# Hymba block with PEER experts: gates applied to more blocks at each build, more activations computed ahead, the mixer's output projection by pairs of tiles

## The chip, the cores and the metric

The kernel runs on one core of a Trainium2 chip. The metric is the time of one execution on the device, in microseconds (us). Times shown are medians of a few runs; the profile is of one execution.

## What is computed

One decoder layer on 512 tokens of width 1024, in float32:

```
h = rmsnorm(x);  z = h @ w_in                 # columns of 4 gated-delta heads and 4 mLSTM heads
mixed = concat(gated_delta(z), mlstm(z))      # each causal, by chunks; 8 heads of 128
x = x + mixed @ w_out                         # the mixer's output projection
h = rmsnorm(x);  x = x + attention(h @ wq, keys(mem), values(mem)) @ wo      # 4 heads, 256 memory tokens
h = rmsnorm(x)                                # PEER: 128*128 experts of one neuron each
q = h @ pwq                                   # 8 heads, two halves of 128 each
per head: scores of both halves against 128 keys, the top 16 of each half, the top 16 of the sums
gate = softmax(the 16 scores)                 # 8*16 = 128 experts for each token
x = x + sum(gate * gelu(h . u[expert]) * v[expert])
out = rmsnorm(x)
```

## The kernel before, in words

The 512 tokens are four tiles of 128. The stages follow each other: the mixer over all four tiles, its output projection (`residual(tiles, hs, "wout")`), cross-attention (`xattn`), and PEER. From the projection on, the order in which code is emitted is a string, ORDER_XA, whose words are run by the loop near the end of the file: `n` norms, `q` query blocks, `s` and `x` the attention's softmax and mix, `o` its output, `i` the norm and queries of PEER, `f` and `u` scores, `r R t T` routing (top 16), `k` and `b B` what follows routing, `p5` five gathered rows, `a2` two activations ahead. Each engine then keeps its own queue, in order.

A projection (`proj`) loads a weight tile of 128x1024 (512 KB) into one of two buffers, splits it into a high part (ACT, line 236) and a low part (DVE line 223 or POOL line 221, by the list `low_on`), and multiplies three times (high by high, high by low, low by high). `projT` is the same with the weights stationary. Where an activation is kept unsplit (`"f"`), the product runs on whole float32 (line 313).

PEER is done in two ways at the same time. Tiles 0 and 1 gather: for each of a token's 128 experts, one indirect DMA on POOL (line 1073) fetches a row of `u` for all 128 tokens (512 KB), and DVE reduces it against the token (line 1100); later the same with rows of `v` (line 1111). That is 512 rows in all. Tiles 2 and 3 are dense: for each of the 128 blocks of 128 experts, PE multiplies by the block of `u` (`pa`, an activation, line 313, then Gelu on ACT, line 972), the result is multiplied by a gate for every expert and token, and PE multiplies by the block of `v` (`o`, line 1000). The rows of the gather, the blocks of `u` (`in_pt`) and those of `v` (`in_pv`) come from HBM.

The gates of the dense tiles are 128 experts x 128 x 256 tokens, mostly zero. `build` makes them for 16 tokens at a time: DVE compares (line 934) and multiplies (line 940), PE multiplies the result (`acc`, line 945), ACT puts it into a `stage` (line 946). There are 16 builds. The dense blocks come in 16 groups of eight, and `room` has place for six groups, so 47 activations (`ahead`, word `a`) can run before the first `o`. After a build, `apply` (line 953) multiplies its gates into the first NOW = 2 groups where they stand; the gates of the other 14 groups are written to a DRAM tensor (`gates_`), and read again in the dense loop, a megabyte a group (line 992), and multiplied there by DVE (line 997).

In the dense loop (`peer_dense`) every step issues the loads of the coming blocks and then runs 3.15 gathered rows while activations are left (ROWS_BOTH), and 2.3 after that (ROWS_DOWN). At the end the gathered tiles are closed first on DVE (lines 1088 to 1091), then the dense ones (lines 1056 to 1066).

Of the kernel before, what the change touches and what calls it, by code (L numbers as in the profile page):

```python
# [6 lines left out]
F32 = mybir.dt.float32  # L7
# [9 lines left out]
P = 128  # L17
# [14 lines left out]
ROWS_BOTH, ROWS_DOWN = 3.15, 2.3  # L32
# [23 lines left out]
ORDER_XA = ("w2 n0 q008 n1 s0 x0 s1 x1 q104 o0 w1 i0 q148 f0 f1 r6 "  # L56
            "f2 s2 p2 f3 s3 p4 x2 p3 r3 p2 r3 k0 x3 p4 o1 p8 i1 e0 R3 p4 R3 p2 R4 k1 "
            "u0 p5 u1 p5 u2 p5 a1 u3 p5 a2 "
            + "t2 p4 a1 " * 4 + "t2 p4 a9 T2 p4 " + "b1 p5 a1 T2 " * 4 + "b1 p5 a8 d0 " + "b1 p5 a2 " * 3
            + "B1 p5 a1 " * 6 + "a1 p5 B1 p5 B1 p5 a6 ")  # L60
# [15 lines left out]
def _body(ctx, tc, A, out, dbg):  # L76
# [245 lines left out]
    def bank():  # L322
        return psB.tile([P, 512], F32, name="acc")

    def bank4():
        return psB.tile([P, 4, P], F32, name="acc")
# [36 lines left out]
    def gates(ph, wk, hs, tiles):  # L363
# [58 lines left out]
        for i in range(n):  # L422
# [8 lines left out]
        return {ti: dict(beta=beta[:, i], cum=cum[:, i], enm=enm[:, i], br=br[:, i], cj=cj[:, i], beg=beg[:, i])  # L431
                for i, ti in enumerate(tiles)}

    def gdn(wk, items, gs, qkv, mixed):
# [15 lines left out]
        bc = bank4()  # L450
        for i, (h, ti) in enumerate(items):
            PE.matmul(bc[:, i], sel[:, h], gs[ti]["br"][:, 0], start=True, stop=True)
            c = gs[ti]["cum"][:, h:h + 1]
            V.scalar_tensor_tensor(ET[:, i], bc[:, i], c, maskT, op0=OP.subtract, op1=OP.add)
            V.scalar_tensor_tensor(EG[:, i], bc[:, i], c, maskP, op0=OP.subtract, op1=OP.add)
# [99 lines left out]
    def mlstm(wk, items, gs, qk, va, mixed):  # L555
# [3 lines left out]
        def wt(name, bufs=1):  # L559
            return wk.tile([P, n, P], F32, name=name, bufs=bufs)  # L560
        ET, es = wt("ET", 2), wt("eg", 2)
        for i, (h, ti) in enumerate(items):
            bc = bank()
            PE.matmul(bc[:, :256], sel[:, h], gs[ti]["br"][:, 1:3].rearrange("p a b -> p (a b)"),
                      start=True, stop=True)
            V.scalar_tensor_tensor(ET[:, i], bc[:, 128:256], gs[ti]["cj"][:, h:h + 1], maskT,
                                   op0=OP.add, op1=OP.add)
            SC.activation(es[:, i], bc[:, 0:128], AF.Exp)
# [30 lines left out]
    def mixer(tiles, aside):  # L599
        nt = len(tiles)  # L600
        with tc.tile_pool(name="mxp", bufs=nt) as ph, tc.tile_pool(name="mxw", bufs=2) as wk:
# [89 lines left out]
            residual(tiles, hs, "wout")  # L691
# [11 lines left out]
    def xattn():  # L703
# [4 lines left out]
        wr = row(1, wpool, name="wh")  # L708
# [18 lines left out]
        def query(g, blocks):  # L727
            def ev(nb, ps):
                SC.activation(qT[:, nb, cols(g)], ps, AF.Copy)
            if "f" in part(g):  # L730
                projected(part(g)["f"], len(g), A["wq"], blocks, ev)
            else:
                projT(part(g), len(g), A["wq"], blocks, ev)
# [187 lines left out]
    NOW = 2  # L921
# [5 lines left out]
    def build(t0, bufs, stage, bank):  # L927

        for s in range(0, TG, TS):
# [9 lines left out]
            for a in range(TS // Q):  # L939
# [3 lines left out]
                for k in range(Q):  # L943
                    for g in range(2):
                        PE.matmul(ps[:, k], oj[:, a, :, k], og[:, g, a, :, k], start=g == 0, stop=g == 1)  # L945
                SC.activation(stage[:, :, s + a * Q:s + a * Q + Q], ps.rearrange("p t i -> p i t"), AF.Copy, scale=1.0 / GSCALE)
        nc.scalar.dma_start(gates_[:, :, t0 // TG].rearrange("g p i t -> p g (i t)"),
                            stage[:, NOW * GB:].rearrange("p (g i) t -> p g (i t)", i=GB))

        def apply():  # L950
            for g in range(NOW):
                a = room[g][:, :, t0:t0 + TG]
                V.tensor_tensor(a, a, stage[:, g * GB:(g + 1) * GB], op=OP.mult)  # L953
        fresh.append(apply)

    fresh = []
# [9 lines left out]
    room, count_a = [], [0]  # L966
# [7 lines left out]
    def peer_dense(wu, psO, psC, rest):  # L974
# [15 lines left out]
        def gates_of(g):  # L990
            if g < NKEY // GB:
                G.dma_start(gb[:, g % 3], gates_[g - NOW])

        def gated(g):

            a = room[g % NROOM].rearrange("p e (c t) -> p c e t", t=TG)
            V.tensor_tensor(a, a, gb[:, g % 3], op=OP.mult)
# [137 lines left out]
    t = late.tile([P, 2, DB, 2 * P], F32R, name="dh0")  # L1135
    dh.append({"h": t[:, 0], "l": t[:, 1]})
    t = late.tile([P, 4, D], F32, name="dh1")
    dh.append({"f": eight(t), "room": t})
# [8 lines left out]
    for a in range(K):  # L1147
        G.memset(rows_[:, 0, a], float(start[a]))
        G.memset(rows_[:, 1, a], float(start[a] - start[a - 1] if a else 0))
        G.memset(rows_[:, 2, a], float(a))  # L1150
# [46 lines left out]
    for what in ORDER_XA.split():  # L1197
# [3 lines left out]
        elif kind == "q":  # L1201
            n, x, y = (int(c) for c in what[1:])
            query(GS[n], range(x, y))
        elif kind == "s":
# [26 lines left out]
        elif kind == "f":  # L1231
            first.scores(n)
        elif kind == "u":
            second.scores(n)
        elif kind == "e":
            t = late.tile([P, 6, D], F32, name="W0")
            room.extend(blocks(t[:, k:k + 2]) for k in (0, 2, 4))
            room.append(blocks(first.room[:, 0:2]))
        elif kind == "d":
            del rings[-6:-2]  # L1240
            room.extend(blocks(more[:, k:k + 2]) for k in (0, 2))
        elif kind == "a":
            ahead(n)
        elif kind == "k":
            ready[G0[n]] = first.finish(G0[n], slot)
        elif kind == "p":
            run(gather, n)
        else:
            if kind not in flows:
                i, f = {"r": (0, 0), "R": (1, 0), "t": (0, 0), "T": (1, 0), "b": (0, 1), "B": (1, 1)}[kind]  # L1250
                g = first if kind in "rR" else second
                flows[kind] = settle(g, g.tiles[i]) if f else g.route(g.tiles[i], spot, 2 if kind == "r" else 1)
            run(flows[kind], n)
# [72 lines left out]
```

## Time and profile before

| | |
|---|---|
| median of 3 runs | 1864.69 us (1860.12 to 1868.1) |
| the profiled execution | 1863.43 us |
| its span, first to last instruction | 1861.5 us |
| mean granted TensorE clock | 0.957 |
| PE busy | 1682.0 us (90%) |
| DVE busy | 1248.2 us (67%) |
| POOL busy | 849.9 us (46%) |
| ACT busy | 393.9 us (21%) |
| moved by DMA | 514.81 MB, mean 277 GB/s |

The busy times are sums over the whole span, in which the stages have different limits: no engine's share says what a stage waits for. For that the view of the windows is read, which gives busy times and the bytes moved in each stretch of the span, and the views of the waits.

### The profile page before, as it was taken

The numbers are of one execution on the slowest core, as the hardware profiler recorded it, in microseconds if no ns is written. First come the engines' busy times: TensorE is split into PE (matmuls) and PEld (weight loads), VectorE is DVE, ScalarE is ACT, GpSimd is POOL, SyncE is SP. The second block draws the span as 40 slices with busy tenths as digits, with TensorE's granted clock in tenths as the row PEclk, the third lists the DMA queues.
The fourth block names the chain that finished last, engine by engine and source line by source line (L and its number), as shares of the span: only waits on it lengthen the run. The fifth ranks groups of instructions, "written<-read, shape, count | busy, mean of one in ns | idle before, by whom it ended". The sixth has DMA issues, their size and how long they took to land.

```text
span 1861.5 us, 21345 instructions
## 1 busy us (share of the span) xinstructions
PE 1682.0 (90%) x7444; PEld 1240.6 (67%) x7444; DVE 1248.2 (67%) x2767; ACT 393.9 (21%) x784; POOL 849.9 (46%) x686
## 2 busy tenths in 40 slices
PE   4999999999799986996998979993899999999993
PEld 3787777787698863885887746662666666664441
DVE  5656655473422598999998876557666566566668
ACT  5433442564243121111222210000000000000000
POOL 2121111323312044567344656666666666666663
PEclk9999999999899988998999979997999999999997
DMA  4111111234524477999799999999999999999996
GB/s 138 63 57 35 57 40 46 69 102 149 168 88 162 149 261 269 350 335 372 259 332 408 367 385 410 410 410 410 410 410 410 409 410 409 410 409 409 409 411 257
DMA packets 165355, 514.81 MB, mean 277 GB/s; under 512 B 15616, under 2 KB 44416, under 8 KB 163456
## 3 DMA queue, kind: packets, MB, share of 16 engines
q0 software_dynamic: 76608, 286.30, 39.3%
q1 hardware_dynamic: 59712, 212.48, 30.9%
q10 hardware_dynamic: 28928, 14.68, 2.7%
q8 instruction: 58, 0.95, 0.2%
q14 instruction: 49, 0.40, 0.1%
HBM read 494.52 MB, written 18.87 MB: 276 GB/s over the span
## 4 chain that ended last, share of the span: by engine, by line
DMA 38%; PE 33%; DVE 19%; issue 4%; POOL 3%; ACT 2%; SPq 0%; DVEq 0%; POOLq 0%; ACTq 0%
PE pj L313 7%; PE pj L271 7%; DMA row<-in_pv,ids 7%; PE pj L284 6%; DMA W<-in_pv,ids 6%; DMA Vm<-in_pv,ids 5%; PE acc L445 4%; DMA row<-in_pu,ids 3%; DMA wl<-in_pv,ids 3%; DMA W<-gates__132 3%; PE acc L945 2%; DMA gates__132<-W 2%; DVE W L1100 2%; DMA wl<-in_pu,ids 2%; DMA KT<-in_pv,ids 1%
## 5 line engine op out<-in xcount | busy, mean ns | idle before, releaser
L1000 PE MATMUL o<-ld,W 128*128 128x512 f32 x832 | 370.9, 596 | 4.6 <-DVE W L953 4.6
L313 PE MATMUL pa<-dh,ld 128*128 128x256 f32 x1296 | 295.5, 381 | 34.7 <-ACT dh L972 34.2
L313 PEld LDWEIGHTS pa<-dh,ld 128*128 128x128 f32 x1296 | 247.3, 191 | 103.1 <-issue 38.2
L1000 PEld LDWEIGHTS o<-ld,W 128*128 128x128 f32 x832 | 158.8, 191 | 175.7 <-issue 167.3
L221 POOL TENSOR_TENSOR wl<-w,wh 128x1024 fp32r<-128x1024 f32 x38 | 92.4, 2434 | 348.8 <-ACT wh L236 294.7
L313 PE MATMUL pj<-dh,w 128*128 128x256 f32 x704 | 161.3, 383 | 0.0
L313 PEld LDWEIGHTS pj<-dh,w 128*128 128x128 f32 x704 | 133.4, 193 | 17.8 <-ACT dh L294 0.3
L1073 POOL DMA_INDIRECT W<-in_pu,ids x73 | 95.4, 1307 | 91.0 <-DVE W L1100 52.2
L1111 DVE SCALAR_TENSOR_TENSOR dh<-row,act,dh 128x1024 f32<-128x1024 f32 x72 | 92.5, 1284 | 53.8 <-DMA row<-in_pv,ids 53.5
L1073 POOL DMA_INDIRECT row<-in_pu,ids x74 | 98.5, 1331 | 64.4 <-issue 17.8
L1073 POOL DMA_INDIRECT row<-in_pv,ids x74 | 99.9, 1351 | 47.2 <-issue 17.9
L313 PE MATMUL pj<-dh 128*128 128x256 f32 x496 | 113.2, 383 | 0.0
L284 PE MATMUL pj<-hT,wh 128*128 128x512 f32 x320 | 111.9, 421 | 0.0
L972 ACT ACTIVATE W<-pa 128x256 f32<-128x256 f32 x65 | 25.0, 384 | 407.2 <-PE pa L313 397.5
L271 PE MATMUL pj<-wh,hT 128*128 128x512 f32 x320 | 106.1, 404 | 0.4 <-ACT hT L211 0.4
L1100 DVE SCALAR_TENSOR_TENSOR row<-row,dh 128x1024 f32<-128x1024 f32 x74 | 88.3, 1223 | 22.4 <-DMA row<-in_pu,ids 22.1
L313 PEld LDWEIGHTS pj<-dh 128*128 128x128 f32 x496 | 94.5, 193 | 12.6
L1100 DVE SCALAR_TENSOR_TENSOR W<-W,dh 128x1024 f32<-128x1024 f32 x73 | 88.4, 1221 | 17.2 <-DMA W<-in_pu,ids 17.2
L236 ACT ACTIVATE wh<-w 128x1024 fp32r<-128x1024 f32 x56 | 59.3, 1059 | 124.2 <-PE pj L271 64.1
L1000 PE MATMUL o<-ld,dh 128*128 128x512 f32 x192 | 85.2, 592 | 0.0
L1073 POOL DMA_INDIRECT wl<-in_pu,ids x41 | 56.6, 1380 | 49.1 <-DVE tv L783 18.6
L1073 POOL DMA_INDIRECT wh<-in_pu,ids x40 | 54.2, 1354 | 49.9 <-DVE wh L1100 22.3
(431 smaller groups left out, 3106.5 us busy)
## 6 DMA issues: line engine op xcount, KB each, us to landing
ld<-in_pv SPq DMA_DIRECT2D x128, 512.0 KB, 6.8
ld<-in_pt SPq DMA_DIRECT2D x81, 512.0 KB, 6.9
gates__132<-W ACTq DMA_DIRECT2D x16, 896.0 KB, 13.9
W<-gates__132 POOLq DMA_DIRECT2D x14, 1024.0 KB, 17.1
w<-in_pt SPq DMA_DIRECT2D x24, 512.0 KB, 6.9
dh<-in_pt SPq DMA_DIRECT2D x23, 512.0 KB, 6.9
w<-in_win SPq DMA_DIRECT2D x20, 512.0 KB, 3.5
w<-in_pwq SPq DMA_DIRECT2D x16, 512.0 KB, 4.7
```

Of the source, the lines that this page charges most:

```text
L221: G.tensor_tensor(out, a, hi, op=OP.subtract)
L236: SC.activation(hi, wt, AF.Copy)
L271: PE.matmul(acc[i], a[:, d, i * P:(i + 1) * P], b[:, z], start=d == 0 and m == 0, stop=d == DB - 1 and m == len(pairs) - 1)
L284: PE.matmul(acc[:, :n * P], a[:, d], b[:, d], start=d == 0 and m == 0, stop=d == DB - 1 and m == 2)
L313: PE.matmul(ps, w[:, d], h[:, d], start=d == 0, stop=d == DB - 1)
L445: PE.matmul(ps[:, i], l[:, i], r[:, i], start=True, stop=True)
L945: PE.matmul(ps[:, k], oj[:, a, :, k], og[:, g, a, :, k], start=g == 0, stop=g == 1)
L972: SC.activation(place(e), ps, AF.Gelu)
L1000: PE.matmul(outs[DENSE[i]][z], place(e)[:, i * P:(i + 1) * P], v[:, z * 512:(z + 1) * 512], start=e == 0, stop=e == NKEY - 1)
L1073: G.indirect_dma_start(out=row, out_offset=None, in_=A[table], in_offset=bass.IndirectOffsetOnAxis(ap=ids[:, s:s + 1], axis=0))
L1100: V.scalar_tensor_tensor(row, row, 1.0, hn, op0=OP.mult, op1=OP.mult, accum_out=act[ti][:, s:s + 1])
L1111: V.scalar_tensor_tensor(hn, row, w, hn, op0=OP.mult, op1=OP.add)
```

## The change

What it does, piece by piece:

- The mixer's output projection runs for tiles 0 and 1 and then for tiles 2 and 3, with the weights loaded and split once for each pair; all low parts there are made by DVE.
- The norm's weight row in `xattn` comes by POOL's queue into a part of another tile, no longer by SP's.
- The query of tiles 2 and 3 is projected with split operands (`projT`) like that of tiles 0 and 1, and stands before the word `i0`.
- The 48 memsets of `row_numbers` move from the start of `xattn` to the word `f0`.
- 24 activations are called for before the first build (16 before); rows are called for six at a build (five before), and 169 in all before the last `apply` is done (158 before).
- `apply` multiplies a build's gates into every group whose eight activations are there: three groups, then four, then five, where it was two. Only what is not applied is written to `gates_` and read again, 188 pieces of 64 KB each way, where it was 224.
- In the mixer, one matmul for all four tiles spreads a head's gate row (line 452 of before) where there were four, and two where there were four of double width (line 564); one Exp stands for four.
- ROWS_BOTH and ROWS_DOWN become 3.1 and 2.1.

```diff
-ROWS_BOTH, ROWS_DOWN = 3.15, 2.3
+ROWS_BOTH, ROWS_DOWN = 3.1, 2.1
...
-ORDER_XA = ("w2 n0 q008 n1 s0 x0 s1 x1 q104 o0 w1 i0 q148 f0 f1 r6 "
+ORDER_XA = ("w2 n0 q008 n1 s0 x0 s1 x1 q104 o0 w1 q148 i0 f0 f1 r6 "
...
-            + "t2 p4 a1 " * 4 + "t2 p4 a9 T2 p4 " + "b1 p5 a1 T2 " * 4 + "b1 p5 a8 d0 " + "b1 p5 a2 " * 3
-            + "B1 p5 a1 " * 6 + "a1 p5 B1 p5 B1 p5 a6 ")
+            + "t2 p4 a2 " * 4 + "t2 p4 a6 T2 p4 a7 " + "b1 p6 a2 T2 " * 4 + "d0 " + "b1 p6 a2 " * 4
+            + "B1 p6 a1 " * 2 + "B1 p6 " * 6 + "a5 ")
...
         bc = bank4()
+        PE.matmul(bc[:, :n], sel[:, items[0][0]], gs["br"][:, :, 0], start=True, stop=True)
         for i, (h, ti) in enumerate(items):
-            PE.matmul(bc[:, i], sel[:, h], gs[ti]["br"][:, 0], start=True, stop=True)
...
-            residual(tiles, hs, "wout")
+            low_on[:] = [V]
+            for k in range(0, nt, 2):
+                residual(tiles[k:k + 2], {z: t[:, :, k * P:(k + 2) * P] for z, t in hs.items()}, "wout")
...
-        wr = row(1, wpool, name="wh")
+        wr = row_(1, up[:, 5], G)
...
-            if "f" in part(g):
-                projected(part(g)["f"], len(g), A["wq"], blocks, ev)
-            else:
-                projT(part(g), len(g), A["wq"], blocks, ev)
+            projT(part(g), len(g), A["wq"], blocks, ev)
...
-    NOW = 2
+    NOW = 3
...
-        nc.scalar.dma_start(gates_[:, :, t0 // TG].rearrange("g p i t -> p g (i t)"),
-                            stage[:, NOW * GB:].rearrange("p (g i) t -> p g (i t)", i=GB))
+
+        n = count_a[0] // GB
+        for g in range(n, NKEY // GB):
+            held[g] = t0 // TG + 1
+        nc.scalar.dma_start(gates_[n - NOW:, :, t0 // TG].rearrange("g p i t -> p g (i t)"),
+                            stage[:, n * GB:].rearrange("p (g i) t -> p g (i t)", i=GB))
 
         def apply():
-            for g in range(NOW):
-                a = room[g][:, :, t0:t0 + TG]
-                V.tensor_tensor(a, a, stage[:, g * GB:(g + 1) * GB], op=OP.mult)
+            for g, k, t in wide:
+                k = min(n - g, k) * GB
+                if k > 0:
+                    a = t[:, :k, t0:t0 + TG]
+                    V.tensor_tensor(a, a, stage[:, g * GB:g * GB + k], op=OP.mult)
...
-                G.dma_start(gb[:, g % 3], gates_[g - NOW])
+                G.dma_start(gb[:, g % 3, :held[g]], gates_[g - NOW, :, :held[g]])
```

Three places show how instructions stand on an engine before and after.

**DVE in the mixer's output projection.** `x<-pj` (line 699, then 700) adds a finished block of a tile to the residual, `wl<-w,wh` (line 223) is the low part of a weight tile. Before:

```order
L212 TENSOR_TENSOR hT<-tr,hT 128x4x128 x8
L223 TENSOR_TENSOR wl<-w,wh 128x1024
L699 TENSOR_TENSOR x<-pj,x 128x512 x4
L223 TENSOR_TENSOR wl<-w,wh 128x1024
L699 TENSOR_TENSOR x<-pj,x 128x512 x4
```

After:

```order
L212 TENSOR_TENSOR hT<-tr,hT 128x4x128 x5
L223 TENSOR_TENSOR wl<-w,wh 128x1024 x2
L700 TENSOR_TENSOR x<-pj,x 128x512
L223 TENSOR_TENSOR wl<-w,wh 128x1024
L700 TENSOR_TENSOR x<-pj,x 128x512
L223 TENSOR_TENSOR wl<-w,wh 128x1024 x3
L700 TENSOR_TENSOR x<-pj,x 128x512
```

The low parts, most of which POOL made before, now stand on DVE between the additions, four for each block of a pair, the first of them behind an addition that waits for PE.

**The norm's weight row, between the projection and the queries.** `wl<-w,wh` (line 221) belongs to the projection, `W<-w,W` and `W<-wl,W` to the query's weights, `in_nrow` is a norm's weight row. Before, POOL has the 48 memsets at this place, and the weight row is on SP's queue, ahead of a load of the query's weights:

```order
L246 DMA w<-in_wout 128x1024 x6
L246 DMA w<-in_wq 128x1024 x2
L246 DMA wl<-in_wq 128x1024
L191 DMA wh<-in_nrow 128x1024
L246 DMA wl<-in_wq 128x1024
```

After, on POOL:

```order
L221 TENSOR_TENSOR wl<-w,wh 128x1024 x11
L191 DMA W_4067<-in_nrow 128x1024
L221 TENSOR_TENSOR W_4065<-w,W_4065 128x1024
L221 TENSOR_TENSOR W_4065<-wl,W_4065 128x1024
L221 TENSOR_TENSOR W_4065<-w,W_4065 128x1024
```

The memsets are gone from here; a load has come in their place, into memory that the projection's operands held until then.

**DVE at the builds.** `KT` and `Vm` are a build's operands, `W<-W,W` is `apply`, `act<-…` is a gathered row. Before, two builds apart by five rows:

```order
L953 TENSOR_TENSOR W_5757<-W_5757,W_4107 128x8x16 x2
L940 TENSOR_TENSOR Vm<-Vm,slot 128x2x512 x2
L1100 SCALAR_TENSOR_TENSOR row,act_5297<-row,dh_4764 128x1024
L1100 SCALAR_TENSOR_TENSOR wh,act_5297<-wh,dh_4764 128x1024
L1100 SCALAR_TENSOR_TENSOR wl,act_5297<-wl,dh_4764 128x1024
L1100 SCALAR_TENSOR_TENSOR wh,act_5297<-wh,dh_4764 128x1024
L1100 SCALAR_TENSOR_TENSOR wl,act_5297<-wl,dh_4764 128x1024
```

After, at the first builds:

```order
L957 TENSOR_TENSOR W_5913<-W_5913,W_4067 128x24x16
L938 TENSOR_TENSOR Vm<-Vm,slot 128x2x512 x2
L932 TENSOR_TENSOR KT<-ioq,slot 128x1024 x2
L932 TENSOR_TENSOR Vm<-ioq,slot 128x1024
L938 TENSOR_TENSOR KT<-KT,slot 128x2x512 x2
L932 TENSOR_TENSOR Vm<-ioq,slot 128x1024
L957 TENSOR_TENSOR W_5913<-W_5913,W_4067 128x24x16
L938 TENSOR_TENSOR Vm<-Vm,slot 128x2x512 x2
L932 TENSOR_TENSOR KT<-ioq,slot 128x1024
```

Before, 80 rows stand ahead of the first build and 155 ahead of the last; after, 102 and 165, and the first four builds have no row between them. Each `apply` is one instruction on three groups (128x24x16) and, later, one or two more on one group. On PE, 24 activations stand ahead of the first build's transposes where there were 16, and behind the last `o` that is mixed with builds there follow four builds with nothing between, where there were two.

## Rows read from the trace of the kernel before

**Rows 1.** Windows: us, busy us of PE, PEld, DVE, ACT, POOL, granted clock, DMA share, GB/s.
```profile
800.00:850.00 50.00, 50.00 (x241) 44.24 (x240) 50.00 (x223) 6.55 (x16) 31.39 (x31) 1.00 0.95 357
...
1250.00:1300.00 50.00, 23.99 (x80) 14.82 (x78) 36.96 (x58) 0.70 (x2) 33.74 (x29) 0.78 1.03 410
...
1650.00:1700.00 50.00, 50.00 (x137) 25.73 (x136) 31.74 (x25) 1.15 (x3) 34.94 (x27) 1.00 1.03 409
```

**Rows 2.** DMA traffic from 1100 to 1815 us.
```profile
DMA packets 78220, 292.28 MB, mean 409 GB/s; under 512 B 8671, under 2 KB 8735, under 8 KB 76397
```

**Rows 3.** Waits of PE, then of ACT, from 1100 us to the end: total, times, longest.
```profile
PE pa L313 <- ACT dh L972: 34.2, 1, 34.2
```
```profile
ACT act L1080 <- DVE row L1100: 50.4, 1, 50.4
```

**Rows 4.** Timeline of the end: start us, us, engine, line, operation, shapes.
```profile
1825.47 4.46 PE L1000 MATMUL o<-ld,dh 128*128 128x512 f32 x10
...
1842.17 1.28 DVE L1111 SCALAR_TENSOR_TENSOR dh<-wl,act,dh 128x1024 f32<-128x1024 f32 x1
...
1849.52 2.48 DVE L1056 TENSOR_TENSOR ld<-o,ld 128x512 f32<-128x512 f32 x4
```

**Rows 5.** Line 564: duration ns min/median/max, first and last start.
```profile
L564 PE MATMUL acc<-br,sel x32: 374/374/478, 347.6 to 413.7; 4*128 4x256 f32 x32
```

**Rows 6.** Chain of work in the output projection: start us, us, what.
```profile
452.05 41.77 PE pj L271 x179
```

**Rows 7.** Chain of work from 405 to 447 us, where weights are split.
```profile
439.04 3.59 DMA w<-in_wout
442.73 1.07 ACT wh L236
```

**Rows 8.** Timeline behind the output projection.
```profile
493.85 1.06 ACT L197 ACTIVATE W<-x 128x1024 f32<-128x1024 f32 x1 [10.15 <-PE pj L271]
...
499.46 3.33 DVE L199 SCALAR_TENSOR_TENSOR W<-x,nr,wh 128x1024 f32<-128x1024 f32 x1
...
502.89 1.94 PE L209 MATMUL tr<-UI,W 128*128 128x128 f32 x8 [9.08 <-issue]
```

**Rows 9.** Split query of tiles 0 and 1 (line 284), then whole-float32 projections on the timeline, two blocks each.
```profile
L284 PE MATMUL pj<-dh,W x192: 278/283/580, 508.6 to 532.3; 128*128 128x256 f32 x192
```
```profile
597.86 7.07 PE L313 MATMUL pj<-dh,W 128*128 128x256 f32 x32
604.77 7.07 PE L313 MATMUL pj<-dh,w 128*128 128x256 f32 x32
```

**Rows 10.** DVE by line and form, 440 to 1105 us: busy us, mean ns.
```profile
L1100 DVE SCALAR_TENSOR_TENSOR W<-W,dh 128x1024 f32<-128x1024 f32 x59 | 71.3, 1220 | 8.5 <-DMA W<-in_pu,ids 8.5
...
L934 DVE TENSOR_TENSOR Vm<-ioq,slot 128x1024 f16<-128x1024 f16 x32 | 21.9, 688 | 8.0 <-PE acc L945 8.0
...
L699 DVE TENSOR_TENSOR x<-pj,x 128x512 f32<-128x512 f32 x16 | 10.9, 687 | 35.4 <-PE pj L271 35.4
L953 DVE TENSOR_TENSOR W<-W,W 128x128 f32<-128x128 f32 x32 | 8.1, 291 | 1.5 <-ACT W L946 1.5
...
L223 DVE TENSOR_TENSOR wl<-w,wh 128x1024 fp32r<-128x1024 f32 x3 | 3.7, 1225 | 10.2 <-ACT wh L236 10.2
```

**Rows 11.** Chain of work: four gathered rows, each with the read of its sum.
```profile
1059.37 4.58 DVE row L1100 x8
```

**Rows 12.** Waits of DVE, 640 to 880 us, then 880 to 1095 us.
```profile
DVE W L1100 <- DMA W<-in_pu,ids: 8.5, 4, 5.9
DVE row L1100 <- DMA row<-in_pu,ids: 6.2, 3, 3.7
```
```profile
DVE Vm L934 <- PE acc L945: 8.0, 5, 2.9
```

**Rows 13.** PE's wait for the first build, from the waits of 640 to 1100 us.
```profile
PE tr L319 <- ACT ijf L906: 13.1, 1, 13.1
```

**Rows 14.** One window, 873.6 to 1092.1 us: all engines; PE on line 945; PE on line 313.
```profile
873.60:1092.10 218.50, 194.26 (x1086) 167.72 (x1086) 197.91 (x412) 54.21 (x104) 110.87 (x80) 0.94 0.97 348
```
```profile
873.60:1092.10 218.50, 66.41 (x512) 58.47 (x512) 0.94 0.97 348
```
```profile
873.60:1092.10 218.50, 127.36 (x544) 103.99 (x544) 0.94 0.97 348
```

**Rows 15.** DMA traffic from 650 to 900 us.
```profile
DMA packets 24219, 76.87 MB, mean 307 GB/s; under 512 B 2336, under 2 KB 5642, under 8 KB 24203
```

## What the change will do to the time

> **What bounds the kernel now.** I read the windows first, then the waits of each engine in the stretches that the windows set apart, then the timeline at the places that the change touches. The windows show three regimes behind the mixer. Up to about 1090 us DVE is the busy engine: in the window 800 to 850 it has 50.00 us of 50, while the DMA engines still have room (share 0.95, 357 GB/s) [rows 1]. From 1100 to 1815 us the DMA engines are full: 292.28 MB at 409 GB/s [rows 2], the share is 1.03 even where PE stands still (1250 to 1300) [rows 1]. PE comes close behind: 50.00 of 50 at 1650 to 1700 [rows 1], and it loses 34.2 us in one wait, behind a Gelu that ACT's queue holds back, since ACT itself waits 50.4 us for a gathered row [rows 3]. At the end PE's last `o` is done at 1829.9 (1825.47 + 4.46), the last gathered row at 1843.5 (1842.17 + 1.28), and DVE turns to the dense tiles' `o` at 1849.5, behind the close of the gathered ones [rows 4]. So the rows end last, and PE could be 19.6 us later without harm.
>
> The sum therefore has three parts: what shifts the start of PEER, what shifts the end of the builds, and what is left to transfer behind them.
>
> **Ahead of PEER.** *Mixer.* 32 matmuls of 374 ns on line 564 become 16 of double width [rows 5], and 32 of line 452 become 8 of fourfold. No row shows the wide form on four partitions. If the wide one costs as much as the narrow, line 564 alone saves 16 x 0.374 = 6.0 us of PE; if it costs as its width, nothing. Heads wait for each other's chains on DVE and ACT as much as for PE, so I take -2, between 0 and -8.
>
> *Output projection.* 179 matmuls take 41.77 us, 0.233 each [rows 6]. A weight tile serves 24 of them now and 12 after, 2.80 us. With two buffers, a buffer is free again after load, high and low part: 3.59 + 1.07 [rows 7] + 1.23 on DVE [rows 10] = 5.89 us for two tiles, 2.95 for one. Sixteen tiles then cost 16 x 0.15 = 2.4 us more than PE's work. At three borders between blocks the low part also stands behind an addition (0.69) that waits for the tile ahead: 0.69 + 1.23 [rows 10] less the other tile's six matmuls (1.4) is 0.5 each, 1.6 in all. I take +4; the bounds are 0 (loads run far enough ahead) and +8 (twice as much).
>
> By the Trainium skill (DMA: Bandwidth & Descriptors, Anatomy of one DMA) a transfer costs about 2.0 us plus its bytes at 436 GB/s, which gives an estimate of 3.2 us for 512 KB, where the row has 3.59. The cycle would be 5.5 us, 2.75 for a tile, PE would not wait for loads, and the +4 would be 1.6.
>
> *The norm behind it.* That tiles 0 and 1 are projected first looks as if their norm could run beside tiles 2 and 3. But ACT's square of the norm is released by PE's last matmul [rows 8], because its output lies over memory that the projection reads, and that is so after the change too. So the 9.08 us in which PE stands [rows 8] stay. The weight row is now loaded only behind that matmul, but the multiplication that needs it starts at 499.46 [rows 8], 5.6 us after it, and a load of that size takes 3.59 [rows 7]. I take 0, between -2 (the memsets are gone from POOL's queue) and +3 (POOL issues late).
>
> *Query of tiles 2 and 3.* Split, eight blocks take 508.6 to 532.6, 24.0 us; in whole float32, two blocks start 6.91 apart, so eight are 27.6 [rows 9]. That is -3.6; the bound is 0, if the additional low parts come late. Together: -2 + 4 + 0 - 3.6 = -1.6.
>
> **Up to the first build.** 102 rows instead of 80 stand ahead of it on DVE. Four take 4.58 us [rows 11], so 22 are 25.2. DVE does wait for rows here, 8.5 + 6.2 us [rows 12], but more rows cannot fill a wait for rows. PE gets eight more activations, 8 x 3.45 = 27.6 [rows 9], of which 13.1 us lie in its wait for the first build [rows 13]; the 14.5 left are less than 25.2, so DVE sets it: +25.2.
>
> **From the first to the last build.** The window 873.6 to 1092.1 holds it: 218.5 us, DVE busy 197.9 [rows 14]. 67 rows instead of 78 are left up to the last `apply`: -12.6. `apply` was 32 operations of 128x128 at 0.291, and becomes 16 of 128x384 and 20 of 128x128. Between 0.291 and 0.687 for 512 elements [rows 10] the row of 384 would be 0.555: 16 x 0.555 - 12 x 0.291 = +5.4. So DVE's work is 190.7. Its idle time was 20.6, of which PE's `acc` had 8.0 [rows 12]. That part falls away in the later builds, which have six rows between them (6.9 us) and at the end nothing of PE's ahead of them. It comes back in part at the first four, which have no rows: DVE needs 8 x 0.688 [rows 10] + 0.6 = 6.1 us for one, PE 66.41 / 16 = 4.15 and one to two activations of 3.45 [rows 9, 14], 9.3, so up to 13 us of waiting, less the routing of tile 3 that DVE has there. PE as a whole does not bind: 34 activations (544 records by 16) [rows 14] become 26. I take 15 us of idle time: 190.7 + 15 - 218.5 = -12.8, with bounds of 0 and 28 us of idle time, -28 and 0. The last build then ends -1.6 + 25.2 - 12.8 = 10.8 us later than before.
>
> **The dense loop.** 11 rows fewer are left, 5.77 MB, and 36 pieces of 64 KB of gates are not read, 2.36 MB. At 409 GB/s [rows 2] that is 14.1 + 5.8 = 19.9 us off the stretch that the DMA engines fill. PE has no more work than before, but its wait matters: with the rows 19.9 us earlier, its end is the end (19.6 apart [rows 4]) unless the 34.2 us shrink. By the order the Gelu of the gathered weights stands behind 23 activations of the loop where it was 27, which PE reaches 4 x 6.9 = 27.6 us sooner (3.45 for `pa` [rows 9], 3.5 for eight of the ten `o` records in 4.46 [rows 4]); the row that it waits for comes 11 rows and 4 steps' loads (4.2 MB) sooner, 24.4 us. The wait is then 37.4, and the gain 16.7. I take -18, the middle, with bounds of -10 (the wait grows to 44) and -20.
>
> **Sum.** 10.8 - 18 = -7.2 against the profiled execution, 1863.4: 1856.2. It lies 1.3 below the median of the runs shown, well inside their spread, so I say **1856**. What a measurement of this kernel can tell from no change is about 0.5%, 9.3 us.
>
> **Rivals.** *The builds give everything back.* DVE waits for PE in the first builds, and nowhere less: idle time 28 instead of 15. Then 10.8 + 13 - 18 = +5.8, 1869. For it: four builds without rows, and the transposes behind 24 activations. Against it: DVE had only 8.0 us of such waits [rows 12] with 34 activations among the builds, and there are 26 now.
>
> *The rows don't come in time (slower).* 76.87 MB came from 650 to 900 us, at 307 GB/s [rows 15]. 22 rows and 8 blocks of `u` more are 15.7 MB. At that rate they take 51 us, not 25.2: +26, 1882. It decides (1873) from 17 us on, that is, if the rate stays below 317 GB/s. For it: DVE does wait for rows there. Against it: the waits are 14.7 us in all [rows 12], and the engines give 409 where they are asked for it [rows 2]; DVE sets the pace in that stretch.
>
> *The change gains more.* If DVE finds its work always ready, idle time falls to about 3, and the end is 12 us earlier: 1844. If the pair did free the norm, PE would keep up to 9.08 us [rows 8]: 1847; the release of the square speaks against it.
>
> *PE's wait grows.* Each us beyond 37.4 is a us of the end; at 44 it is 1863.
>
> **How the numbers follow.** The forecast, 1847 to 1865 by the bounds of its small terms, has 0.45, and I put half of it on either side of 1855.4. The builds giving back has 0.22 (1862 to 1875, the growing wait with it), the late rows 0.13, the greater gain 0.20 (1836 to 1848). Faster by over 0.5%: 0.20 + 0.23 = 0.43; slower: 0.13 + 0.02 = 0.15; within: 0.42. The range that leaves out no more than 2 in 10 is 1838 to 1878.
>
> **What would show it.** In the changed profile: the output projection some 4 us longer, and PE's stop behind it again about 9; the query of tiles 2 and 3 near 24 us; the first build's transposes some 24 us later than 873.6, with PE's wait ahead of them about as long as before; the last `apply` near 1103; the dense stretch still at 409 GB/s and some 18 us shorter; PE's wait for the held Gelu near 37 us and beginning earlier after the builds' end. I am wrong if DVE waits much longer for rows ahead of the first build, if the projection doubles its waits, or if DVE stands at the first builds for over 20 us.

## The result, and the profile after

Nine runs of the changed kernel have a median of 1858.03 us (1852.99 to 1863.05), nine of the kernel before beside them 1868.1 (1860.12 to 1877.14). The ratio is 0.9947, 95% interval 0.9925 to 0.9969: about 10 us faster. The two profiled executions lie much closer together, 1863.43 and 1861.86, since the one lies below all but one of the nine runs of before and the other above all but one of the nine of the change. So the traces show where time went, and the ratios how much it was.

The way to read the two traces is by landmarks, events that every version has: the last transposes of the mixed heads, the last addition of the output projection, the first gathered row, the last `apply`, and the first addition of the dense tiles' `o`, behind which nothing changes. Each is the first or last start of a line in the trace.

| stretch, us | before | after | difference | prediction's term |
|---|---|---|---|---|
| mixer, to its last transposes | 451.8 | 440.4 | -11.4 | -2 |
| output projection | 42.1 | 50.0 | +7.9 | +4 |
| to the first gathered row | 174.1 | 170.3 | -3.8 | -3.6 |
| to the last `apply` | 424.1 | 450.9 | +26.8 | +25.2 - 12.8 |
| to the dense additions | 757.4 | 736.5 | -20.9 | -18 |
| sum | 1849.5 | 1848.1 | -1.4 | -7.2 |

The signs are right and two sizes, the mixer's and the builds', are far off, one in each direction. Each column is one execution, and part of the mixer's difference is the clock (see the last section). The lines of the changed trace that answer to the rows of before follow.

The whole mixer of the kernel before (busy us of PE, PEld, DVE, ACT, POOL, clock, DMA share, GB/s), then the change's spreading matmuls, those of the delta heads (line 451) and of the mLSTM heads (line 564): ns min/median/max, first and last start:

```profile
0.00:451.80 451.80, 409.86 (x2299) 331.48 (x2300) 266.28 (x711) 203.54 (x386) 101.66 (x59) 0.98 0.23 75
```
```profile
L451 PE MATMUL acc<-br,sel x8: 587/640/692, 61.9 to 261.7; 4*128 4x512 f32 x8
```
```profile
L564 PE MATMUL acc<-br,sel x16: 587/587/692, 338.3 to 402.8; 4*128 4x512 f32 x16
```

The double width costs 587 where the single cost 374 [rows 5]: neither the same nor twice as much. PE was busy for 409.9 of the 451.8 us before.

The output projection, waits from 436 to 490 us, and its loads from the page:

```profile
ACT wh L236 <- DMA w<-in_wout: 23.9, 11, 3.3
...
PE pj L271 <- ACT wh L236: 2.8, 2, 2.5
```
```profile
w<-in_wout SPq DMA_DIRECT2D x16, 512.0 KB, 3.8
```

ACT now waits for eleven of the sixteen loads: the pairs run at the pace of load and split, and PE stands 2.5 us at the start, before the first pieces are there. Behind the projection, two of the loads in flight from 490.66 to 499.06 us (KB, us to landing) and the timeline:

```profile
wh<-in_nrow SPq DMA_DIRECT2D x1, 512.0 KB, 8.4
W<-in_nrow POOLq DMA_DIRECT2D x1, 512.0 KB, 8.4
```
```profile
490.37 1.06 ACT L197 ACTIVATE W<-x 128x1024 f32<-128x1024 f32 x1 [4.18 <-PE pj L271]
...
499.08 1.28 DVE L199 SCALAR_TENSOR_TENSOR W<-x,nr,W 128x1024 f32<-128x1024 f32 x1 [0.63 <-DMA W<-in_nrow]
...
500.47 1.94 PE L209 MATMUL tr<-UI,W 128*128 128x128 f32 x8 [10.13 <-issue]
```

The square is still released by PE's last matmul and PE stands 10.13 us, 1.05 more than before [rows 8]. The weight row takes 8.4 us and is now what comes last. It is not POOL's queue that is slow: another norm's row, sent by SP 0.15 us earlier, takes 8.4 too, and from 490.66 to 499.06 us the core moves 324 GB/s with its DMA engines busy for 0.95 of the time. The 1.05 is the difference of two larger numbers. The multiplication starts 8.71 us behind the start of the square where it was 5.61, 3.1 later; but it takes 1.28 us where it took 3.33 [rows 8]. In all six profiles with the weight row's old queue it takes 3.33, beside a 2.3 us split of a weight tile on POOL, and in all eight others 1.28, with nothing on POOL beside it.

The builds: windows from the first row to the last `apply`, before and after (busy us of PE, PEld, DVE, ACT, POOL, clock, DMA share, GB/s); waits of DVE there, after; PE's from 900 to 1112; POOL's longest from 895 to 955.

```profile
668.00:1092.10 424.10, 364.07 (x1844) 302.98 (x1842) 392.49 (x1168) 94.04 (x194) 231.00 (x189) 0.93 0.92 336
```
```profile
660.70:1111.90 451.20, 363.95 (x1845) 303.24 (x1844) 411.29 (x1195) 94.23 (x194) 243.45 (x200) 0.89 0.91 327
```
```profile
DVE row L1104 <- DMA row<-in_pu,ids: 10.7, 4, 9.0
DVE W L1104 <- DMA W<-in_pu,ids: 8.7, 5, 5.8
```
```profile
DVE Vm L932 <- PE acc L943: 12.4, 7, 4.4
```
```profile
PE acc L943 <- DVE KT L938: 45.6, 4, 23.1
```
```profile
POOL row L1077 <- DVE W L869: 28.2, 1, 28.2
```

DVE's work is as predicted: 18.8 us more in the whole stretch, and `apply` on 384 elements takes 0.564 where 0.555 was interpolated. But its idle time went up by 8.3 us, from 31.6 to 39.9. It waits 14.9 us for PE's `acc` (12.4 of them in the line above) where it was 8.4, and 19.4 for rows where it was 17.7. These 19.4 lie ahead of the builds, where it was 11.0; among the builds, where it was 6.7, it waits for no row. The 14.7 us of [rows 12] take in a part of each.

A window at the first builds (columns as above); then the dense loop: traffic from 1100 to 1815 us, PE's longest wait from 1100 us on, and the end.

```profile
900.00:950.00 50.00, 38.93 (x236) 35.29 (x237) 45.23 (x88) 11.90 (x22) 12.10 (x10) 0.86 0.79 249
```
```profile
DMA packets 79446, 290.86 MB, mean 407 GB/s; under 512 B 8686, under 2 KB 10094, under 8 KB 78005
```
```profile
PE pa L313 <- ACT W L976: 31.6, 1, 31.6
```
```profile
1839.44 6.17 PE L1004 MATMUL o<-ld,dh 128*128 128x512 f32 x14
...
1848.07 2.48 DVE L1060 TENSOR_TENSOR ld<-o,ld 128x512 f32<-128x512 f32 x4
```

The stretch is still full, at 407 GB/s, and 20.9 us shorter. PE's last `o` ends at 1845.6, 2.5 us ahead of the dense additions, where it had 19.6 us to spare [rows 4]. The window 900 to 950 is new: at the first builds, which have no rows between them, the transfers fall to 249 GB/s, where the windows from 850 to 1000 us had 309 to 363 before. PE stands 23.1 us, up to 911.1, until DVE has the first build's operands, and while the four builds run POOL's next row waits 28.2 us for DVE, up to 941.3.

### The profile page after: what moved, and what is told of

It is laid out like the page before. It is cut to its first block, busy times and chain, and to the rows that moved or that the text cites. A ratio compares the mean times of both kernels' runs of the same rounds, so it can differ in the third digit from the quotient of the medians.

```text
span 1860.1 us, 21460 instructions
## 1 busy us (share of the span) xinstructions
PE 1671.3 (90%) x7468; PEld 1233.1 (66%) x7468; DVE 1268.5 (68%) x2792; ACT 407.1 (22%) x786; POOL 839.6 (45%) x684
## 3 DMA queue, kind: packets, MB, share of 16 engines
q1 hardware_dynamic: 60720, 216.15, 31.6%
## 4 chain that ended last, share of the span: by engine, by line
DMA 37%; PE 30%; DVE 19%; issue 8%; POOL 4%; ACT 2%; SPq 0%; DVEq 0%; POOLq 0%; ACTq 0%
DMA row<-in_pv,ids 8%; PE pj L284 7%; DMA W<-in_pv,ids 6%; PE pj L271 5%; PE pj L313 5%; PE acc L445 4%; DMA wl<-in_pv,ids 3%; DMA row<-in_pu,ids 3%; DMA KT<-in_pv,ids 3%; DVE W L1104 3%; DMA Vm<-in_pu,ids 2%; PE acc L943 2%; DMA W<-in_pu,ids 2%; DMA Vm<-in_pv,ids 2%; DMA gates__132<-W 2%
## 5 line engine op out<-in xcount | busy, mean ns | idle before, releaser
L313 PE MATMUL pa<-dh,ld 128*128 128x256 f32 x1296 | 294.8, 380 | 32.1 <-ACT W L976 31.6
L221 POOL TENSOR_TENSOR wl<-w,wh 128x1024 fp32r<-128x1024 f32 x32 | 77.0, 2410 | 307.7 <-ACT wh L236 246.7
L313 PE MATMUL pj<-dh,w 128*128 128x256 f32 x640 | 144.9, 382 | 1.0 <-ACT W L976 0.8
L1077 POOL DMA_INDIRECT row<-in_pu,ids x75 | 96.1, 1281 | 104.2 <-DVE W L869 28.2
L313 PEld LDWEIGHTS pj<-dh,w 128*128 128x128 f32 x640 | 121.0, 192 | 17.6 <-ACT W L976 1.2
L1077 POOL DMA_INDIRECT row<-in_pv,ids x74 | 101.5, 1372 | 50.2 <-issue 18.8
L1104 DVE SCALAR_TENSOR_TENSOR W<-W,dh 128x1024 f32<-128x1024 f32 x72 | 86.9, 1222 | 17.7 <-DMA W<-in_pu,ids 17.7
L236 ACT ACTIVATE wh<-w 128x1024 fp32r<-128x1024 f32 x64 | 67.7, 1058 | 109.8 <-PE pj L271 31.7
L1077 POOL DMA_INDIRECT wh<-in_pu,ids x41 | 59.0, 1439 | 46.5 <-DVE wh L1104 25.0
L1077 POOL DMA_INDIRECT wl<-in_pu,ids x42 | 51.4, 1224 | 50.9 <-PE pj L313 17.9
```

The costliest lines, as they stand in the source:

```text
L221: G.tensor_tensor(out, a, hi, op=OP.subtract)
L236: SC.activation(hi, wt, AF.Copy)
L313: PE.matmul(ps, w[:, d], h[:, d], start=d == 0, stop=d == DB - 1)
L1077: G.indirect_dma_start(out=row, out_offset=None, in_=A[table], in_offset=bass.IndirectOffsetOnAxis(ap=ids[:, s:s + 1], axis=0))
L1104: V.scalar_tensor_tensor(row, row, 1.0, hn, op0=OP.mult, op1=OP.mult, accum_out=act[ti][:, s:s + 1])
```

## The experiments

The theory behind most of them is that what comes ahead of PEER shifts the end one for one, the builds hold DVE and the loop behind them holds the transfers, so that each part's price adds up. Its rivals are named with each run. Ratios are to the kernel before in the same set of runs; the landmarks of every profile are in the table behind the last run.

**The whole projection.** The change with one projection over four tiles.

```diff
-            low_on[:] = [V]
-            for k in range(0, nt, 2):
-                residual(tiles[k:k + 2], {...}, "wout")
+            residual(tiles, hs, "wout")
```

> The changed kernel with the output projection over all four tiles again. In the profile of the change the stretch from the last transposes of the mixed heads to the last matmul of the projection is 50.0 us, before it was 42.1. Theory: what stands ahead of PEER shifts everything behind it, so the pairs cost about 8 us of the end; this run is 6 to 8 us faster than the change (ratio to the kernel before about 0.991), its stretch is about 42 us and the first gathered row comes some 8 us earlier. Rival: the loop behind is held by the transfers of its rows, and rows that start earlier only queue; then the last row ends within 2 us of the change's.

Ratio 0.9926 (0.9900 to 0.9953), median 1849.76. The projection takes 41.6 us and the first row comes 7.0 us earlier than in the change. But this profile's builds took 455.4 us, and the last row ends only 2.3 us earlier, so it alone does not refute the rival; the ratio moved by 4 us, where 6 to 8 were expected. The runs with the old builds settle it.

**The old builds.** The change with the order, NOW, `apply` and ROWS of before.

> The changed kernel with the order of builds, rows and activations, NOW, the width of apply and the two ROWS numbers of the kernel before; the rest of the change stays. Theory of the prediction: the order and the wide apply lose 15 to 25 us up to the last build and win about 20 behind it, so this part is worth about 0 to 5 us, and the run is 4 to 8 us faster than the kernel before (ratio 0.996 to 0.998), through the earlier start of PEER alone. Rival: the build part is the gain and the rest is worth nothing; then the run is level with the kernel before (ratio 1.000).

Ratio 0.9937 (0.9911 to 0.9962). From the first row to the dense additions 1180.6 us, as before (1181.5), where the change has 1187.4. The start is 11.2 us earlier than before and arrives in full, and the builds of the change add nothing to it; the rival falls. The gain is larger than the 4 to 8 us expected, since the mixer's part is.

**The mixer's edit alone**, on the kernel before (both hunks of the diff that concern `bc`).

> The kernel before with only the mixer's new spreading of gate rows (one matmul for four tiles, one Exp for four). The trace of the change has the last transposes of the mixed heads 11.4 us earlier. Theory: that comes from this edit alone and passes through, so the run is 9 to 11 us faster than the kernel before (ratio about 0.995) and the last transposes start near 440 us instead of 451.7. Rival, the prediction's size: 2 us, ratio 0.999.

Ratio 0.9919 (0.9890 to 0.9948). The last transposes are at 439.3, 12.5 earlier, the first row 12.1, the dense additions 11.4. One edit that the prediction priced at 2 us gives as much as the whole change. How much of it is the clock is taken up with its halves.

**Activations later.** The change with 17 activations ahead of the first build; NOW goes with it, since only two groups are then full.

```diff
-"t2 p4 a6 T2 p4 a7 " + "b1 p6 a2 T2 " * 4 + "d0 "
+"t2 p4 a6 T2 p4 " + "b1 p6 a2 T2 " * 4 + "a7 d0 "
-    NOW = 3
+    NOW = 2
```

> The changed kernel with 17 activations called for ahead of the first build instead of 24 (the seven come after the fourth build) and NOW = 2, so that four builds apply to two groups. By the order 81 gathered rows then stand ahead of the first build instead of 100, and six between any two builds. 192 pieces of gates are written and read instead of 188. Theory: the first builds without rows between them cost DVE waits and leave the transfers idle (249 GB/s from 900 to 950 us); spread, the last apply comes 5 to 10 us earlier and the run is 4 to 8 us faster than the change (ratio 0.990 to 0.993). Rival: the sum of DVE's work and of the bytes is the same, and so is the time, within 2 us of the change.

Ratio 0.9913 (0.9877 to 0.9949). The window at the first builds, to set beside that of the change:

```profile
900.00:950.00 50.00, 50.00 (x269) 44.69 (x268) 46.83 (x104) 10.65 (x23) 26.53 (x16) 1.00 0.94 338
```

PE is full and the transfers go on at 338 GB/s. The stretch up to the last `apply` is 444.9 us, 6.0 less than in the change, and the dense loop as short (735.3). The ratios differ by 6 us too, though their intervals overlap. That is the size the theory gave, but not quite its way: DVE's waits for PE are 15.3 us, no less than the change's 14.9, and those for rows fall from 19.4 to 14.5.

**The kernel before again**, for a second profile.

> The kernel before, unchanged, for a second profile of it. Where one execution differs from the next by chance, its landmarks show by how much: in the first profile the mixed heads' last transposes are at 451.7 us, the first gathered row at 668.0, the last apply at 1092.1. If the mixer's 11 to 15 us between the kernels are chance, this profile has them near 440; if they are the edit's, it has them within 3 us of 451.7.

453.8, 669.9 and 1093.7 us: within 2.1 us of the first profile at each. By these two the mixer's 12 us are not chance; but the run with the builds alone, whose mixer has the same code, has 444.4, so a part of them is (see the halves).

**Whole projection and old builds.** What is left of the change are the mixer's edit, the split query, the weight row and the memsets.

> The changed kernel with the whole output projection and the builds, order and apply of the kernel before: what is left of the change are the mixer's edit, the split query, the weight row's queue and the memsets. Theory: whatever comes ahead of PEER shifts the end one for one. The mixer's edit alone gave about 12 us, the pairs cost 8, so this run's first gathered row is near 649 and its time 6 to 8 us under the run with old builds and pairs, near 0.988 of the kernel before. Rival: with an earlier start the rows wait for transfers, and it is level with the mixer's edit alone (0.992).

Median 1841.97, ratio 0.9906 (0.9871 to 0.9941). The first row is at 645.7, and the dense additions follow 1178.9 us later, no longer than in any run with old builds, so an earlier start is not lost to the transfers. That is read from the traces; the ratio cannot be told from the rival's 0.992. Pairs cost 7.8 us (49.4 against 41.6). The split query, with the weight row's cost in it, gives some 4 (174.0 to 175.3 us from the projection to the first row without it, 169.5 to 171.1 with it).

**No held Gelu.** The change with the Gelu of the gathered weights kept in program order.

```diff
-            SC.activation(act[ti], act[ti], AF.Gelu)
+            tc.keep_in_program_order(SC.activation(act[ti], act[ti], AF.Gelu))
```

> The changed kernel with the Gelu of the gathered weights kept in program order on ACT, so that it stands behind 67 activations of the dense loop instead of 23 and no longer holds the queue. Theory: the stretch is filled by transfers, PE's wait of 31.6 us is the other side of them; the wait at this place goes, PE waits elsewhere instead or ends earlier, and the time is within 3 us of the change. Rival: PE's wait is lost time, since PE's last product (1845.6) and the last row (1842.0) end together in the change; then the run is over 5 us faster than the change.

Median 1856.18, ratio 0.9965 (0.9944 to 0.9987), level with the change. PE's last records of `o`:

```profile
1799.66 7.89 PE L1004 MATMUL o<-ld,dh 128*128 128x512 f32 x18
```

The wait of 31.6 us is gone (PE's only one from 1100 us on is 6.0), PE is done at 1807.6 instead of 1845.6, and the stretch is 736.0 us instead of 736.5. Here, PE's wait in a stretch that the transfers fill cost nothing.

**The wide apply alone**, on the whole projection with old builds.

> The run with the whole projection and old builds, plus the wide apply alone: each build's gates go at once into as many groups as have their activations (two at first, then three, four and five), with the order of rows and activations of the kernel before. Theory of the prediction's terms: DVE gets some 3 to 5 us more work up to the last build, and about 2 MB fewer are read behind it (5 us), so the two cancel within 2 us. Rival: DVE's waits in the builds hide the wider operations, and it is 4 to 6 us faster than without them.

Median 1841.08, ratio 0.9891 (0.9857 to 0.9926), level with the run without it. In this one profile the builds take 9.9 us more and the dense loop 5.0 less. That it cancels holds for the time; whether the builds' 9.9 are the wide operations or partly chance, one profile cannot tell.

**Halves of the mixer's edit**, each on the kernel before.

> The kernel before with the one wide matmul for the gate row in the gated-delta heads alone. The two profiles of the kernel before have the mixed heads' last transposes at 451.7 and 453.8 us, six profiles with the whole edit at 434.6 to 441.5. Theory: PE's work is the bound of the mixer, and the edit takes 32 records of 128 columns down to 8 of 512, some 4 us of busy time; the last transposes come 4 to 8 us earlier than in the kernel before. Rival: the gain is all in the mLSTM heads, with their chain through DVE and ACT, and this run is level with the kernel before.

> The kernel before with the two wide matmuls and the single Exp in the mLSTM heads alone. Theory: 32 records of 374 ns become 16 of 587, under 3 us of PE; what is left of the 12 to 17 us would come from the chain through DVE and ACT, one operation of ACT in place of four for each head. If PE's work alone decides, the last transposes come 2 to 4 us earlier; if the chain decides, 8 to 12.

Gated-delta heads alone: ratio 0.9936 (0.9906 to 0.9966), last transposes at 439.9. mLSTM heads alone: 0.9963 (0.9931 to 0.9994), last transposes at 453.1, as before. In the traces it is all the delta heads' part, 12 to 14 us where 4 to 8 were expected (4.5 against the 444.4 of the run with the builds alone); the times put 7 us in the other half. PE's clock says why the numbers scatter. In the window 130 to 150 us (PE busy, granted clock, DMA share, GB/s), the kernel before again, and the run with the builds alone, whose mixer is that of before:

```profile
130.00:150.00 20.00, 19.49 (x60) 0.58 0.16 53
```
```profile
130.00:150.00 20.00, 19.06 (x102) 1.00 0.17 52
```

The mean granted clock of every execution is on record. Over the 75 of the kernel before beside these runs, a straight line gives 1.8 us for each 0.001 of it, with a scatter of 3.8 us. Set against that line at their own clocks, the delta heads' edit is worth about 9 us, the mLSTM heads' 2 and both together 10. This is an estimate, but it agrees with the traces on which half it is, and makes the edit's 15 us by the ratio partly clock.

**The builds alone**, on the kernel before.

> The kernel before with the change's builds alone: its order of rows, activations and builds, NOW, the wide apply and the two ROWS numbers. From the first gathered row to the end of the dense loop five profiles with the old builds took 1177.7 to 1181.0 us, three with the change's 1186 to 1191. Theory: this part of the change loses 5 to 9 us, ratio 1.003 to 1.005. The prediction's terms for it (25.2 - 12.8 - 18) had it win 5.6, ratio 0.997.

Ratio 1.0017 (0.9979 to 1.0054): no gain, and no loss that can be told from none. In the trace the stretch from the first row is 1195.6 us, 14 more than before: 457.7 up to the last `apply`, 737.9 behind it. The prediction's 0.997 is outside the interval.

**Spread builds with the whole projection.**

> The whole output projection with the spread builds (17 activations ahead of the first build, six rows between any two): the run with old builds and whole projection differs from it by 11 rows moved ahead of the last apply and by the wide apply. Theory: a row costs DVE as much in the builds as it frees of transfers behind them, and the stretch from the first gathered row is 1177 to 1181 us again, the time within 3 us of that run (ratio about 0.989). Rival: with no bunching the moved rows and the unread gates win their 20 us of transfers for less, and it is over 5 us faster.

Median 1841.9, ratio 0.9867 (0.9815 to 0.9918). 440.7 up to the last `apply`, 20.0 more than with the old builds, and 734.9 behind it, 23.3 less: 1175.6 in all. That is 3 us less than with the old builds. The times do not settle theory against rival: the medians are level (1841.9 and 1842.0), the ratios (0.9867 and 0.9906) lie 7 us apart, and their intervals overlap. Against the same projection with the bunched builds (0.9926) it is 11 us, and 16.4 in the trace. By their ratios the three kernels near 1842 beat the change by 8 to 15 us.

The landmarks of all profiles, us (stretches as in the first table; the last column is from the first row to the dense additions):

| kernel | mixer | projection | to row | to `apply` | to the additions | sum of the last two |
|---|---|---|---|---|---|---|
| before | 451.8 | 42.1 | 174.1 | 424.1 | 757.4 | 1181.5 |
| before again | 453.8 | 42.1 | 174.0 | 423.8 | 757.5 | 1181.3 |
| mLSTM half | 453.1 | 41.6 | 174.3 | 423.6 | 758.2 | 1181.8 |
| builds alone | 444.4 | 42.1 | 175.2 | 457.7 | 737.9 | 1195.6 |
| delta half | 439.9 | 42.1 | 175.3 | 422.9 | 759.4 | 1182.3 |
| mixer's edit | 439.3 | 41.6 | 175.0 | 424.5 | 757.7 | 1182.2 |
| old builds | 436.9 | 49.4 | 170.5 | 420.7 | 759.9 | 1180.6 |
| whole, old builds | 434.6 | 41.6 | 169.5 | 420.7 | 758.2 | 1178.9 |
| wide apply | 434.9 | 41.6 | 170.5 | 430.6 | 753.2 | 1183.8 |
| the change | 440.4 | 50.0 | 170.3 | 450.9 | 736.5 | 1187.4 |
| whole projection | 441.5 | 41.6 | 170.6 | 455.4 | 736.6 | 1192.0 |
| no held Gelu | 434.9 | 49.1 | 171.1 | 451.5 | 736.0 | 1187.5 |
| activations later | 437.8 | 49.5 | 170.5 | 444.9 | 735.3 | 1180.2 |
| spread, whole | 440.0 | 41.6 | 170.5 | 440.7 | 734.9 | 1175.6 |

## Why the prediction was right, and where its steps were not

1856 and 1858 agree, but by errors that cancel: the mixer gave 9 us more than its term, the builds cost 14 more, and the projection and the dense loop were off by 4 and 3 in opposite directions. The sum starts from 1863.4, where the nine runs of before have 1868.1; from there its -7.2 would give 1860.9. That the number came out so closely is luck.

**The mixer (-2, between 0 and -8).** This term was mis-sized: nine profiles with the edit end the mixer between 434.6 and 441.5 us. Without it, two profiles have 451.8 and 453.8, and 444.4 where the clock held. Alone it is worth 15 us by its ratio and about 10 at equal clock. Two steps failed. The sentence that heads wait as much for DVE and ACT as for PE was not read from a row; PE was busy for 409.9 of 451.8 us up to the last transposes, and the work taken from it counted. And line 452, from 32 matmuls to 8, was named and never priced: its busy time falls from 8.4 to 4.5 us, that of line 564 from 9.5 to 7.9. These 5.5 us are about half of the gain at equal clock; the chain that gives the other half is not shown.

**The output projection (+4).** Right in mechanism, half in size: +7.9. The cycle of load, high and low part is 3.8 + 1.06 + 1.23 = 6.1 us for two tiles, 0.25 a tile over PE's 2.80, so 3.9 for sixteen. PE stands 2.5 us at the start, which the sum left out; with the 1.6 of the borders that is 8.0. The load of 512 KB took 3.8, not the 3.59 of one alone. By the Trainium skill's fit (DMA: Bandwidth & Descriptors, Anatomy of one DMA), which the page gives for DMAs that GpSimd issues, it would have been an estimated 3.2 and PE would not have waited; the trace, where SP issues the load, does not agree.

**The norm (0) and the query (-3.6).** Both held. The pairs free nothing, as the release of the square said. The weight row, expected within 3.59 as if alone, took 8.4 among other loads; it came 3.1 us late, of which a shorter multiplication gave 2.05 back. The query gave some 4.

**Up to the first build (+25.2) and on to the last (-12.8).** Together +12.4; measured +26.8 in the change, +27 to +34 in three other profiles with its builds. The work was right: DVE's busy time grew by 18.8 us, and the sum had 25.2 - 12.6 + 5.4 = 18.0. The failed step is the idle time: taken at 15 us among the builds, 5.6 less than before, it was 20.5 there (212.9 us from 899 to 1111.9, DVE busy 192.4), and over the whole stretch it grew by 8.3. The prediction did count up to 13 us of waiting for PE at the first four builds, but set most of it against the routing of tile 3: its 15 leaves 2.4 beside the 12.6 us (20.6 less the 8.0 of [rows 12]) that were not waits for `acc`. DVE's waits for PE came to 14.9. And ahead of the first build the sum had no more waiting for rows, where it rose from 11.0 to 19.4. With the builds in a row no gathered row is used meanwhile, POOL's next one waits 28.2 us, and the transfers fall (249 GB/s). With spread builds the stretch is 444.9 and 440.7 us, with bunched ones 450.9 to 457.7 in four profiles, and DVE is idle for 35 and 31 us against 40 to 46. What is left, 17 to 20 us, is DVE's work.

**The dense loop (-18).** -20.9, near the 19.9 of the bytes. PE's wait did not grow to 37 us, and the run without it shows that the 31.6 us did not matter: PE's end, though only 2.5 us ahead of the dense additions, was still ahead.

**What the builds' part is worth.** The prediction had it gain 5.6; by its run alone (1.0017) it gains nothing. Bunched, eleven rows and the wide `apply` cost the builds somewhat more than they free behind; spread, about as much (20.0 against 23.3): work moves from the stretch that the transfers hold into the one that DVE holds. So the change's gain is that of the mixer and the query, less the pairs.

**Rivals.** The one that the builds give everything back was the true one for that part; it named the waiting at the first builds, and its condition, 7.4 us more idle time than before, was met by 8.3 over the whole stretch. The late rows were a part of it: DVE waited 8.4 us longer for rows ahead of the first build, where that case had 26. That the pairs free the norm was rightly set low.

## What to carry to other kernels

Price the stretch that nobody looks at: a small edit can count in a stage where one engine is busy nine tenths of the time, however short its instructions, so price every line that it touches. Moving work between two stages pays only by the difference of their limits; write down both prices before moving it, and keep it spread, since a bunch makes both engines and the queue behind them wait. A long wait of an engine beside a full transfer was free here, since that engine still ended ahead of the other, so look at how far apart the ends are, not at the wait.

## What the hardware showed

In the kernel before, TensorE's granted clock fell to 0.50, the lower level of 1.2 GHz, for 10 us of the mixer in the first profile (134.7 to 144.9 us; mean 0.74 from 130 to 150) and for 17 us in the second (133.2 to 150.2; 0.58). In the second, PE had worked at the full clock from 100 to 132.3 us with one stop of 0.21 us, and then waited 0.51 us for ACT; behind that it was busy throughout, at the lower clock. In the run with the builds alone, whose mixer has the same code, it waited 0.52 us at the same place and kept the full clock, and its mixer ended 7 to 9 us sooner (444.4). With the mixer's edit, or the delta heads' part of it, the window had 0.83 to 1.00. So of the 10 to 19 us between the mixers with and without the edit some 8 are the clock, where it falls, and the rest is the edit. Why the same code keeps it in one execution and not in another stays open; that the edit makes the fall less likely is argued from fourteen profiles, not shown.
